# Gathered rows used one block later, mixer outputs normed per head, and a PSUM copy on ScalarE in the output projection

## The chip, the cores and the metric

The kernel runs on one core of a Trainium2 chip. A core has five engines, each with its own in-order instruction queue: TensorE (PE) multiplies matrices into PSUM, VectorE (DVE) and GpSimd (POOL) work elementwise, ScalarE (ACT) applies functions and casts, SyncE (SP) mostly issues transfers. Sixteen DMA engines move data between HBM and SBUF. The metric is the device time of one execution in microseconds (us); less is better.

## The reference

One decoder block with 512 tokens of width 1024, all in float32:

```python
h = rmsnorm(x, norm1_w) * (1 + sc1) + sh1                 # adaLN from c
qa, ka, va, qm, km, vm, om, ip, fp, ga, gm = split_cols(h @ w_in)
y_a = rmsnorm(diff_attention(qa, ka, va), subln_w) * 0.8  # 8 heads of 128
y_m = rmsnorm(mlstm(qm, km, vm, ip, fp), ml_norm_w) * sigmoid(om)   # 8 heads of 128
x = x + gt1 * ((sigmoid(ga) * y_a + sigmoid(gm) * y_m) @ w_out)
h2 = rmsnorm(x, norm2_w) * (1 + sc2) + sh2
x = x + gt2 * peer_ffn(h2, ...)
return rmsnorm(x, final_norm_w)

def peer_ffn(h, w_q, sub_keys, U, V):     # 128 x 128 = 16384 experts
    # 8 heads; the two best-16 lists of product keys give 16 experts for each head
    act = gelu(U[idx] . h)                # one neuron for each of the 8 x 16 picks
    return sum(gate * act * V[idx])
```

## The kernel before

A float32 product is computed as three products of rounded parts: ACT rounds a tile to `hi`, DVE (or POOL) subtracts to get `lo` (`split`, L137 and L138), and PE adds hi x hi, lo x hi and hi x lo in PSUM (`mm3`, L187 to L189).

**The mixers.** Four passes, `hp` = 0 to 3, each compute two heads (`u` = 0, 1) of both mixers. Attention leaves `y_a`, the mLSTM leaves `y_m`, 128 tokens by 256 columns for each of four token tiles `t`. While ACT squares them it collects sums of squares in `ssq`. Then `rstd` turns `ssq` into `rs` (L118 on DVE, a power on POOL at L119), sixteen multiply-multiply instructions (L699, L701) apply `rs` and the gates, and one add (L703) merges the two mixers into `mrg`.

**The output projection.** `merged_t` transposes `mrg` through PE (`mTp`, L601) into `mT`, one k tile for each head. In the last pass, `out_begin` projects k tiles 0 to 5 before that pass's own merge: for each half `j` of the columns and each token tile `t`, a group of 18 matmuls (`wo`) into one PSUM bank of a ring of two, then `o_res = wo * gt1` on DVE (L618) and `x += o_res` on POOL (L619). `out_end` adds k tiles 6 and 7, the last pass's heads. The weights `wo{k}_{j}` are split with their `lo` part on POOL.

**The expert layer.** Scores, top-16 lists and routing tables keep DVE busy from 640 to 940 us. After that, all 16384 experts are computed densely for tokens 128 to 511, in 128 blocks `n1` of 128 experts: a U block (`act`, 24 matmuls of 384 columns, L1000 to L1002), then gelu and the product with the routing weights `W` (`ga`, L1031), and a V block (`y`, 18 matmuls of 512 columns, L1046). Tokens 0 to 127 take the other way: 256 indirect transfers of 512 KB gather the rows that each token picked, 128 of U and then 128 of V. DVE uses a gathered U tile in a dot product (`junk`, L931) and a gathered V tile in an accumulation (`yg`, L941). I call the stretch up to about 1405 us, in which U rows are gathered, the U stretch, and the one from there to 1905 us the V stretch.

**What sets the order.** A scheduler orders the instructions on each engine before the kernel runs; at run time each engine follows its list strictly. Two pins matter here. Each block's gathers are issued on POOL (L925) behind a one-column copy `pace` (L994) that reads that block's `lo_U`, so they start when DVE has made `lo_U` (L992). And a gather needs one of five buffers of the tag `g`, so it waits until DVE has used the tile five gathers back. Each of the `hi` and `lo` weight tiles has two buffers.

Of the kernel before, what the change touches and what calls it, by code (L numbers as in the profile page):

```python
# [61 lines left out]
def block_kernel(ctx: ExitStack, tc: tile.TileContext, a, out, dbg=None):  # L62
# [380 lines left out]
    def attention(hp, y, ssq, between=None):  # L443
# [13 lines left out]
        for u in range(2):  # L457
            if u and between:
                between()
            h = 2 * hp + u  # L460
            us = slice(u * P, (u + 1) * P)

            halves = slice(0, 64), slice(64, P)
            for nm, src in (("q", q_sb), ("k", k_sb)):
                ps = tr_tile(f"{nm}T{h}")
                for t in range(NT):
                    T.transpose(ps[:, t * P:(t + 1) * P], src[:, t, us], ident)
                if nm == "q":
                    for c, r in enumerate(halves):
                        split(qz[0][r, c], qz[1][r, c], ps[r])  # L470
                else:
                    kh, kl = [lp.tile([P, S], F32R, tag=f"kT_{n}", bufs=QB, name=f"kT_{n}") for n in ("hi", "lo")]
                    split(kh, kl, ps)
            rinv = lp.tile([P, NT, 2], F32, tag="rinv", bufs=2, name="rinv")
            for t in range(NT):
                n = (t + 1) * P
                sc = ps_sc.tile([P, 2, S], F32, tag="sc", name="sc")
                for c in range(2):
                    qs = slice(t * P, (t + 1) * P)
                    T.matmul(sc[:, c, 0:n], qz[0][:, c, qs], kh[:, 0:n], start=True, stop=False)  # L480
# [24 lines left out]
            oT = lp.tile([P, S], F32, tag="t2k", bufs=3, name="oT")  # L505
            A.copy(oT, po)
            pt = tr_tile("pt")
            for t in range(NT):
                T.transpose(pt[:, t * P:(t + 1) * P], oT[:, t * P:(t + 1) * P], ident)
            for t in range(NT):  # L510
                V.tensor_scalar(y[:, t, us], pt[:, t * P:(t + 1) * P], rinv[:, t, 0:1], None, op0=OP.mult)
                A.activation(junk, pt[:, t * P:(t + 1) * P], AF.Square, scale=rinv[:, t, 0:1],
                             accum_out=ssq[:, t, u:u + 1])

    def mlstm(hp, y, ssq):

# [50 lines left out]
        for u in range(2):  # L567
# [21 lines left out]
            V.reciprocal(den, den)  # L589
            for c in range(NT):  # L590
                V.tensor_scalar(y[:, c, us], pn[:, c, 0:P], den[:, c:c + 1], None, op0=OP.mult)
                A.activation(junk, pn[:, c, 0:P], AF.Square, scale=den[:, c:c + 1], accum_out=ssq[:, c, u:u + 1])


    x1h, mT = [], []
# [73 lines left out]
    for hp in range(4):  # L669
        js = slice(hp * 256, (hp + 1) * 256)  # L670
        y_a = mrg[:, :, js]
        y_m = lp.tile([P, NT, 256], F32, tag="y_m", bufs=1, name="y_m")
        ssq, rs = [lp.tile([P, 2, NT, 2], F32, tag=n, bufs=2, name=n) for n in ("ssq", "rs")]
        attention(hp, y_a, ssq[:, 0], gate_chain if hp == 0 else None)
        mlstm(hp, y_m, ssq[:, 1])
        mw = lp.tile([P, 256], F32, tag="mw", bufs=1, name="mw")
        A.dma_start(mw, a["ml_norm_w"][js].partition_broadcast(P))

        def gate(tag, off, name):
            g = lp.tile([P, NT, 256], F32, tag=tag, bufs=1, name=name)  # L680
# [12 lines left out]
        rstd(rs.rearrange("p a t u -> p (a t u)"), ssq.rearrange("p a t u -> p (a t u)"), P, 4 * NT)
        ga4 = ga.rearrange("p t (h d) -> p (t h) d", d=P)
        G.tensor_tensor(ga4, ga4, bc(subw[:, None, :], [P, 2 * NT, P]), op=OP.mult)
        for t in range(NT):
            for u in range(2):
                us = slice(u * P, (u + 1) * P)
                V.scalar_tensor_tensor(ga[:, t, us], y_a[:, t, us], rs[:, 0, t, u:u + 1], ga[:, t, us],  # L699
                                       op0=OP.mult, op1=OP.mult)  # L700
                V.scalar_tensor_tensor(gm[:, t, us], y_m[:, t, us], rs[:, 1, t, u:u + 1], gm[:, t, us],  # L701
                                       op0=OP.mult, op1=OP.mult)
        V.tensor_tensor(mrg[:, :, js], ga, gm, op=OP.add)  # L703
    h2_hi, h2_lo = out_end()
    if "x1" in dbg:
        nc.sync.dma_start(dbg["x1"], x1_dram)
# [219 lines left out]
                             in_offset=bass.IndirectOffsetOnAxis(ap=idx0[:, s:s + 1], axis=0))  # L926
        return t_

    def gather_u(s):
        u = gather(a["U"], s)  # L930
        V.scalar_tensor_tensor(junk2, u, 1.0, hrow, op0=OP.mult, op1=OP.mult, accum_out=act[:, s:s + 1])  # L931
        if s == NS - 1:
            A.activation(act, act, AF.Gelu)
            V.tensor_tensor(act, act, gate0, op=OP.mult)

    def gather_v(s):
        v = gather(a["V"], s)
# [39 lines left out]
        V.scalar_tensor_tensor(idx0[:, gs], idg.rearrange("p h k -> p (h k)"), float(KEYS),  # L977
                               idl.rearrange("p h k -> p (h k)"), op0=OP.mult, op1=OP.add)

    gsteps = [(gather_u, s) for s in range(NS)] + [(gather_v, s) for s in range(NS)]  # L980
    h_hi, h_lo = h2_hi[:, :, d0:d0 + XT], h2_lo[:, :, d0:d0 + XT]

    def gstep(n1):
# [2 lines left out]
    def up(n1):  # L986
# [147 lines left out]
```

## Time and profile before

| what | value |
|---|---|
| three timed runs | 1936.87, 1919.65, 1936.19 us (median 1936.19) |
| the profiled execution | 1931.02 us, span 1929.2 us, mean granted clock of PE 0.978 |
| busy share: PE, DVE, ACT, POOL | 94%, 74%, 42%, 36% |
| chain of work that ended last | PE 58%, DVE 18%, DMA 9%, ACT 5%, issue 5%, POOL 4% |

The shares are averages over stages with different limits, so they are read by stage: between 1100 and 1400 us PE never rests, before 940 us DVE is the busiest engine, and later both wait at times. Idle time in a row is the time that the engine sat before the instructions of that group, and the name behind the arrow is what it waited for last. [...]

### The profile page before, as it was taken

How to read it: one execution, taken by the hardware profiler on the slowest of the kernel's cores; microseconds unless marked ns; L12 is line 12 of the kernel's file. 1: busy time of each engine (PE TensorE's matmuls, PEld its weight loads, DVE VectorE, ACT ScalarE, POOL GpSimd, SP SyncE). 2: the span in 40 equal slices, each digit the busy share in tenths (PEclk: the TensorE clock that was granted, in tenths of full speed). 3: DMA queues.
4: the chain of work that ended last, by engine and by line, in shares of the span. 5: the costliest groups of instructions: out<-in, count | busy, mean ns of one | idle time of the engine just before them, and what ended most of it. 6: DMA issues, size and time to landing. Idle time of an engine off the chain costs nothing.

```text
span 1929.2 us, 28915 instructions
## 1 busy us (share of the span) xinstructions
PE 1814.1 (94%) x10751; PEld 1632.3 (85%) x10751; DVE 1428.4 (74%) x2732; ACT 811.1 (42%) x1359; POOL 685.8 (36%) x608
## 2 busy tenths in 40 slices
PE   5999899899998998999699999999999899999997
PEld 4989799798986888999688888899898788888886
DVE  7664746645556799999889888887776667776777
ACT  5565464463562423555434333333333233333332
POOL 2523325234135310331001664565433433334333
PEclk8999999999999999999799999999999999999999
DMA  8422414314222233366794999999986887787883
GB/s 283 129 69 81 138 59 158 112 63 148 71 88 98 75 102 99 117 239 247 265 302 153 339 355 349 317 337 336 323 285 247 276 299 274 273 295 246 321 283 132
DMA packets 160283, 404.26 MB, mean 210 GB/s; under 512 B 14471, under 2 KB 63368, under 8 KB 160142
## 3 DMA queue, kind: packets, MB, share of 16 engines
q1 hardware_dynamic: 117026, 240.91, 38.6%
q0 software_dynamic: 36864, 134.23, 19.0%
q10 hardware_dynamic: 6252, 27.28, 3.6%
q8 instruction: 84, 1.38, 0.3%
q14 instruction: 57, 0.47, 0.1%
HBM read 373.52 MB, written 28.84 MB: 209 GB/s over the span
## 4 chain that ended last, share of the span: by engine, by line
PE 58%; DVE 18%; DMA 9%; ACT 5%; issue 5%; POOL 4%; SPq 0%; DVEq 0%; POOLq 0%; ACTq 0%
PE y L1046 20%; PE act L1002 7%; PE act L1000 7%; PE act L1001 7%; DMA gath<-V,idx 4%; DMA ada_w<-ada_w 3%; POOL gath L925 2%; DVE lo_U L992 2%; DVE ada_acc L219 1%; DVE lo_V L138 1%; PE wps L876 1%; PE wps L877 1%; DVE ga L699 1%; ACT p L489 1%; DVE gm L701 1%
## 5 line engine op out<-in xcount | busy, mean ns | idle before, releaser
L1002 PE MATMUL act<-h_hi,lo_U 128*128 128x384 f32 x1024 | 347.1, 339 | 16.9 <-DVE lo_U L992 16.7
L1000 PE MATMUL act<-h_hi,hi_U 128*128 128x384 f32 x1024 | 345.0, 337 | 2.6 <-ACT ga L1004 2.2
L1001 PE MATMUL act<-h_lo,hi_U 128*128 128x384 f32 x1024 | 344.3, 336 | 0.0
L994 POOL COPY pace<-lo_U 128x1 f32<-128x1 f32 x128 | 99.9, 782 | 572.8 <-DVE lo_U L992 572.1
L941 DVE SCALAR_TENSOR_TENSOR yg<-gath,act,yg 128x1024 f32<-128x1024 f32 x127 | 163.0, 1283 | 111.2 <-DMA gath<-V,idx 110.6
L1046 PE MATMUL y<-lo_V,ahi 128*128 128x512 f32 x762 | 241.2, 397 | 2.6 <-DVE lo_V L138 2.6
L137 ACT CAST hi_V<-raw_V 128x1024 fp32r<-128x1024 f32 x128 | 134.3, 1050 | 245.9 <-PE y L1046 207.3
L1046 PE MATMUL y<-hi_V,alo 128*128 128x512 f32 x762 | 233.9, 395 | 1.0 <-DVE alo L138 1.0
L1046 PE MATMUL y<-hi_V,ahi 128*128 128x512 f32 x762 | 222.4, 397 | 6.0 <-ACT ahi L137 4.2
L925 POOL DMA_INDIRECT gath<-U,idx x128 | 177.1, 1383 | 130.1 <-DVE junk L931 99.3
L1002 PEld LDWEIGHTS act<-h_hi,lo_U 128*128 128x128 f32 x1024 | 192.8, 188 | 25.3 <-DVE lo_U L992 20.6
L1000 PEld LDWEIGHTS act<-h_hi,hi_U 128*128 128x128 f32 x1024 | 192.9, 188 | 8.5 <-ACT ga L1004 3.1
L1001 PEld LDWEIGHTS act<-h_lo,hi_U 128*128 128x128 f32 x1024 | 192.7, 188 | 4.3
L138 DVE TENSOR_TENSOR lo_V<-raw_V,hi_V 128x1024 fp32r<-128x1024 f32 x128 | 155.8, 1219 | 41.9 <-ACT hi_V L137 39.0
L991 ACT CAST hi_U<-raw_U 128x1024 fp32r<-128x1024 f32 x128 | 134.2, 1049 | 111.4 <-PE act L1001 98.6
L137 ACT CAST ahi<-ga 128x384 fp32r<-128x384 f32 x127 | 65.0, 512 | 271.0 <-DVE ga L1031 140.3
L1046 PEld LDWEIGHTS y<-hi_V,alo 128*128 128x128 f32 x762 | 142.5, 187 | 35.4 <-DVE alo L138 1.9
L1046 PEld LDWEIGHTS y<-lo_V,ahi 128*128 128x128 f32 x762 | 142.8, 188 | 35.0 <-DVE lo_V L138 3.6
L992 DVE TENSOR_TENSOR lo_U<-raw_U,hi_U 128x1024 fp32r<-128x1024 f32 x128 | 156.4, 1222 | 19.4 <-ACT hi_U L991 13.3
L1046 PEld LDWEIGHTS y<-hi_V,ahi 128*128 128x128 f32 x762 | 142.0, 189 | 33.3 <-ACT ahi L137 4.8
L925 POOL DMA_INDIRECT gath<-V,idx x128 | 149.4, 1167 | 35.3 <-issue 31.5
L931 DVE SCALAR_TENSOR_TENSOR junk<-gath,hrow 128x1024 bf16<-128x1024 f32 x128 | 156.0, 1219 | 4.4 <-DMA gath<-U,idx 3.5
(465 smaller groups left out, 4134.2 us busy)
## 6 DMA issues: line engine op xcount, KB each, us to landing
raw_U<-UT SPq DMA_DIRECT2D x128, 512.0 KB
raw_V<-V SPq DMA_DIRECT2D x128, 512.0 KB
ada_w<-ada_w SPq DMA_DIRECT2D x96, 256.0 KB
W_dram<-st ACTq DMA_DIRECT2D x24, 960.0 KB
W<-W_dram SPq DMA_DIRECT2D x60, 384.0 KB
raw_wq<-wq SPq DMA_DIRECT2D x16, 512.0 KB
raw_q<-w_in SPq DMA_DIRECT2D x8, 512.0 KB
raw_k<-w_in SPq DMA_DIRECT2D x8, 512.0 KB
```

Of the source, the lines that this page charges most:

```text
L137: A.copy(hi, src)
L138: eng.tensor_tensor(lo, src, hi.bitcast(F32), op=OP.subtract)
L925: G.indirect_dma_start(out=t_, out_offset=None, in_=src, in_offset=bass.IndirectOffsetOnAxis(ap=idx0[:, s:s + 1], axis=0))
L931: V.scalar_tensor_tensor(junk2, u, 1.0, hrow, op0=OP.mult, op1=OP.mult, accum_out=act[:, s:s + 1])
L941: V.scalar_tensor_tensor(yg, v, act[:, s:s + 1], yg, op0=OP.mult, op1=OP.add)
L991: A.copy(hi, raw)
L992: V.tensor_tensor(lo, raw, hi.bitcast(F32), op=OP.subtract)
L994: with tc.issue_after(G.tensor_copy(pace, lo[:, 0:1].bitcast(F32)).ins):
L1000: T.matmul(ps, hi[:, ks], h_hi[:, k], start=(k == 0), stop=False)
L1001: T.matmul(ps, hi[:, ks], h_lo[:, k], start=False, stop=False)
L1002: T.matmul(ps, lo[:, ks], h_hi[:, k], start=False, stop=(k == KD - 1))
L1046: T.matmul(ys[d][j], l[:, tsl], r[:, j * 512:(j + 1) * 512], start=(m == 0 and i == 0), stop=(m == KEYS - 1 and i == 2))
```

## The change

There are three edits.

1. In the expert layer, the issue of a gather and its use come apart. The gathers of block `n1` are issued where they were, but they go on a list `landing`; the list is emptied, and the tiles are used on DVE, right behind `lo_U` of block `n1 + 1` (pinned behind it by `issue_after`). The buffers of tag `g` go from five to six.
2. The norm and merge of a pass are done head by head. `ssq` and `rs` get the head as their first index; per pass there are two `rstd` on 128x8 in place of one on 128x16, and two adds of 128x4x128 in place of one of 128x4x256. The sixteen multiplies are the same.
3. In the eight groups of `out_begin` (`ks[0] == 0`), ACT copies the PSUM bank to `o_res` in SBUF, and DVE multiplies it there by `gt1`. In `out_end` DVE still reads PSUM.

```diff
-NGB = 5
+NGB = 6
...
         o = lp.tile([P, S], F32, tag="t2k", bufs=3, name="o_res")
+        if ks[0] == 0:
+            A.copy(o, ps)
+            ps = o
         V.tensor_tensor(o, ps, gt1[:, j * 512:(j + 1) * 512], op=OP.mult)
...
-        rstd(rs.rearrange("p a t u -> p (a t u)"), ssq.rearrange("p a t u -> p (a t u)"), P, 4 * NT)
...
-        for t in range(NT):
-            for u in range(2):
-                us = slice(u * P, (u + 1) * P)
-                V.scalar_tensor_tensor(ga[:, t, us], y_a[:, t, us], rs[:, 0, t, u:u + 1], ga[:, t, us],
+        for u in range(2):
+            us = slice(u * P, (u + 1) * P)
+            rstd(rs[:, u].rearrange("p a t -> p (a t)"), ssq[:, u].rearrange("p a t -> p (a t)"), P, 2 * NT)
+            for t in range(NT):
+                V.scalar_tensor_tensor(ga[:, t, us], y_a[:, t, us], rs[:, u, 0, t:t + 1], ga[:, t, us],
...
-        V.tensor_tensor(mrg[:, :, js], ga, gm, op=OP.add)
+            V.tensor_tensor(y_a[:, :, us], ga[:, :, us], gm[:, :, us], op=OP.add)
...
-    def gather_u(s):
-        u = gather(a["U"], s)
+    def use_u(s, u):
...
+    landing = []
...
-        V.tensor_tensor(lo, raw, hi.bitcast(F32), op=OP.subtract)
+
+        with tc.issue_after(V.tensor_tensor(lo, raw, hi.bitcast(F32), op=OP.subtract).ins):
+            while landing:
+                f, s, t_ = landing.pop(0)
+                f(s, t_)
         pace = dp.tile([P, 1], F32, tag="pace", bufs=4, name="pace")
         with tc.issue_after(G.tensor_copy(pace, lo[:, 0:1].bitcast(F32)).ins):
-            for f, s in gsteps[gstep(n1):gstep(n1 + 1)]:
-                f(s)
+            for f, n, s in gsteps[gstep(n1):gstep(n1 + 1)]:
+                landing.append((f, s, gather(a[n], s)))
```

The first place is DVE's list in the V stretch, around block 98. Before, `gath_16251` and `gath_16254` are the two gathers of block 98, issued behind `lo_U98`; `gath_16322` is one of block 99.

```order
L992 TENSOR_TENSOR lo_U98_16245<-raw_U_16243,hi_U98_16244 128x1024
L1031 TENSOR_TENSOR ga_16138<-ga_16138,W0_6501 128x384
L138 TENSOR_TENSOR alo_16149<-ga_16138,ahi_16148 128x384
L992 TENSOR_TENSOR lo_U99_16316<-raw_U_16314,hi_U99_16315 128x1024
L1031 TENSOR_TENSOR ga_16212<-ga_16212,W0_6501 128x384
L138 TENSOR_TENSOR alo_16222<-ga_16212,ahi_16221 128x384
L941 SCALAR_TENSOR_TENSOR yg_9155<-gath_16251,act_9154,yg_9155 128x1024
L941 SCALAR_TENSOR_TENSOR yg_9155<-gath_16254,act_9154,yg_9155 128x1024
L941 SCALAR_TENSOR_TENSOR yg_9155<-gath_16322,act_9154,yg_9155 128x1024
L138 TENSOR_TENSOR lo_V98_16286<-raw_V_16284,hi_V98_16285 128x1024
L941 SCALAR_TENSOR_TENSOR yg_9155<-gath_16325,act_9154,yg_9155 128x1024
L992 TENSOR_TENSOR lo_U100_16386<-raw_U_16384,hi_U100_16385 128x1024
```

So before, the blocks come in pairs, and five instructions stand between `lo_U98` and the first use of its gathers. In the changed kernel the list repeats every three blocks. Here `gath_16342` and `gath_16344` belong to block 99, and `gath_16412`, `gath_16414` and `gath_16416` to block 100.

```order
L996 TENSOR_TENSOR lo_U100_16404<-raw_U_16402,hi_U100_16403 128x1024
L943 SCALAR_TENSOR_TENSOR yg_9175<-gath_16342,act_9174,yg_9175 128x1024
L1042 TENSOR_TENSOR ga_16300<-ga_16300,W0_6521 128x384
L943 SCALAR_TENSOR_TENSOR yg_9175<-gath_16344,act_9174,yg_9175 128x1024
L996 TENSOR_TENSOR lo_U101_16477<-raw_U_16475,hi_U101_16476 128x1024
L138 TENSOR_TENSOR alo_16311<-ga_16300,ahi_16310 128x384
L1042 TENSOR_TENSOR ga_16371<-ga_16371,W0_6521 128x384
L943 SCALAR_TENSOR_TENSOR yg_9175<-gath_16412,act_9174,yg_9175 128x1024
L138 TENSOR_TENSOR alo_16381<-ga_16371,ahi_16380 128x384
L943 SCALAR_TENSOR_TENSOR yg_9175<-gath_16414,act_9174,yg_9175 128x1024
L996 TENSOR_TENSOR lo_U102_16548<-raw_U_16546,hi_U102_16547 128x1024
```

Now six instructions, two of them uses of older gathers, stand between `lo_U100` and the first use of its gathers, and a `yg` follows `lo_U100` at once. POOL's own list, one `pace` and two or three gathers for each block, is as before.

The second place is the output projection. On POOL, before, around the last pass's power (`rs<-rs`):

```order
TENSOR_TENSOR rs<-rs,nhalf 128x16
TENSOR_TENSOR x1_0<-x1_0,o_res 128x512
TENSOR_TENSOR lo_wo2_1<-raw_wo2_1,hi_wo2_1 128x1024
TENSOR_TENSOR lo_wo4_1<-raw_wo4_1,hi_wo4_1 128x1024
TENSOR_TENSOR x1_0<-x1_0,o_res 128x512
```

And on POOL in the changed kernel:

```order
TENSOR_TENSOR rs<-rs,nhalf 128x8
TENSOR_TENSOR x1_0<-x1_0,o_res 128x512
TENSOR_TENSOR x1_0<-x1_0,o_res 128x512
TENSOR_TENSOR rs<-rs,nhalf 128x8
TENSOR_TENSOR lo_wo2_1<-raw_wo2_1,hi_wo2_1 128x1024
TENSOR_TENSOR lo_wo4_1<-raw_wo4_1,hi_wo4_1 128x1024
```

The split of `wo2_1` and `wo4_1`, which PE needs for the second half of the columns, now stands behind the second head's power. On PE, the transposes `mTp` of k tiles 6 and 7 stood together behind the first two groups of the second half; now k tile 6 is transposed six matmuls into the first of these groups, and k tile 7 ten matmuls before the end of the two. On ACT at this place the changed kernel has:

```order
COPY o_res<-wo 128x512
ACTIVATE junk_s,ssq<-pn,den 128x128
CAST hi_wo2_1<-raw_wo2_1 128x1024
CAST hi_wo4_1<-raw_wo4_1 128x1024
COPY o_res<-wo 128x512
CAST mT_hi<-mTp 128x512
CAST hi_wo6_0<-raw_wo6_0 128x1024
CAST mT_hi<-mTp 128x512
COPY o_res<-wo 128x512
```

The copies are new; the fourth one, the second copy of this piece, stands ahead of `hi_wo6_0`.

## Rows read from the trace of the kernel before

**Rows 1.** Windows: busy us (x instructions) of PE, PEld, DVE, ACT, POOL, PEclk, DMA share, GB/s

```profile
1100.00:1400.00 300.00, 300.00 (x1452) 263.66 (x1452) 249.66 (x367) 105.78 (x143) 167.85 (x137) 1.00 0.95 339
```

**Rows 2.** Groups of instructions, 1405 to 1905 us: busy, mean ns | idle before, releasers

```profile
L941 DVE SCALAR_TENSOR_TENSOR yg<-gath,act,yg 128x1024 f32<-128x1024 f32 x127 | 163.0, 1283 | 111.2 <-DMA gath<-V,idx 110.6
L1002 PE MATMUL act<-h_hi,lo_U 128*128 128x384 f32 x465 | 157.8, 339 | 12.9 <-DVE lo_U L992 12.8
...
L925 POOL DMA_INDIRECT gath<-V,idx x128 | 149.4, 1167 | 35.3 <-issue 31.5 <-DVE yg L941 3.8
L1046 PE MATMUL y<-lo_V,ahi 128*128 128x512 f32 x336 | 106.1, 396 | 1.4 <-DVE lo_V L138 1.4
L1046 PE MATMUL y<-hi_V,ahi 128*128 128x512 f32 x339 | 105.4, 395 | 1.2 <-ACT ahi L137 0.7 <-ACT hi_V L137 0.5
...
L994 POOL COPY pace<-lo_U 128x1 f32<-128x1 f32 x57 | 31.3, 550 | 278.0 <-DVE lo_U L992 277.4 <-issue 0.5
```

**Rows 3.** Timeline of DVE, 1526 to 1541 us: start, us, instruction [idle before <-releaser]

```profile
1526.25 1.22 DVE L992 TENSOR_TENSOR lo_U<-raw_U,hi_U 128x1024 fp32r<-128x1024 f32 x1
1527.39 0.55 DVE L1031 TENSOR_TENSOR ga<-ga,W 128x384 f32<-128x384 f32 x1
1527.86 1.28 DVE L941 SCALAR_TENSOR_TENSOR yg<-gath,act,yg 128x1024 f32<-128x1024 f32 x1
1529.05 0.55 DVE L138 TENSOR_TENSOR alo<-ga,ahi 128x384 fp32r<-128x384 f32 x1
1529.52 1.28 DVE L941 SCALAR_TENSOR_TENSOR yg<-gath,act,yg 128x1024 f32<-128x1024 f32 x1
...
1539.34 1.28 DVE L941 SCALAR_TENSOR_TENSOR yg<-gath,act,yg 128x1024 f32<-128x1024 f32 x1 [3.39 <-DMA gath<-V,idx]
```

**Rows 4.** Timeline of POOL over the same stretch and to 1545 us

```profile
1527.54 0.44 POOL L994 COPY pace<-lo_U 128x1 f32<-128x1 f32 x1 [4.30 <-DVE lo_U L992]
1528.14 2.30 POOL L925 DMA_INDIRECT gath<-V,idx  x1 [0.16 <-issue]
...
1544.83 0.94 POOL L925 DMA_INDIRECT gath<-V,idx  x1 [0.30 <-issue]
```

**Rows 5.** Timeline of DVE and POOL at 1442 us

```profile
1441.86 1.28 DVE L941 SCALAR_TENSOR_TENSOR yg<-gath,act,yg 128x1024 f32<-128x1024 f32 x1
1442.01 1.17 POOL L994 COPY pace<-lo_U 128x1 f32<-128x1 f32 x1 [8.57 <-DVE lo_U L992]
```

**Rows 6.** Chain of waits, 1405 to 1905 us: start, us, link; two of eleven

```profile
1464.03 5.14 DMA gath<-V,idx
...
1890.27 8.53 DMA gath<-V,idx
```

**Rows 7.** Timeline of PE, 585 to 600 us, in the output projection

```profile
592.11 0.79 PE L187 MATMUL wo<-hi_wo,mT_hi 128*128 128x512 f32 x1 [4.85 <-DVE o_res L618]
...
597.67 0.40 PE L188 MATMUL wo<-lo_wo,mT_hi 128*128 128x512 f32 x1
597.91 0.40 PE L189 MATMUL wo<-hi_wo,mT_lo 128*128 128x512 f32 x1
```

**Rows 8.** Timeline of DVE, 577 to 593 us

```profile
583.17 2.48 DVE L701 SCALAR_TENSOR_TENSOR gm<-y_m,rs,gm 128x128 f32<-128x128 f32 x1
...
587.97 0.34 DVE L701 SCALAR_TENSOR_TENSOR gm<-y_m,rs,gm 128x128 f32<-128x128 f32 x1
...
591.38 0.68 DVE L618 TENSOR_TENSOR o_res<-wo,gt 128x512 f32<-128x512 f32 x1
```

**Rows 9.** Timeline of POOL, 577 to 593 us

```profile
578.94 2.90 POOL L119 TENSOR_TENSOR rs<-rs,nhalf 128x16 f32<-128x16 f32 x1 [0.56 <-DVE rs L118]
...
583.05 4.84 POOL L138 TENSOR_TENSOR lo_wo<-raw_wo,hi_wo 128x1024 fp32r<-128x1024 f32 x2
```

**Rows 10.** Instructions of one line (the query's L767): ns min/median/max, first and last start

```profile
L767 ACT COPY qt<-pr_wq x16: 575/588/595, 646.3 to 746.4; 128x512 f32<-128x512 f32 x16
```

**Rows 11.** Costliest groups of the page: the uses of gathered U rows

```profile
L931 DVE SCALAR_TENSOR_TENSOR junk<-gath,hrow 128x1024 bf16<-128x1024 f32 x128 | 156.0, 1219 | 4.4 <-DMA gath<-U,idx 3.5
```

More of the change, by code (lines that the diff above doesn't have):

```diff
@@ L512, in attention @@
                 A.activation(junk, pt[:, t * P:(t + 1) * P], AF.Square, scale=rinv[:, t, 0:1],
-                             accum_out=ssq[:, t, u:u + 1])
+                             accum_out=ssq[:, u, t:t + 1])
     def mlstm(hp, y, ssq):
@@ L591, in mlstm @@
                 V.tensor_scalar(y[:, c, us], pn[:, c, 0:P], den[:, c:c + 1], None, op0=OP.mult)
-                A.activation(junk, pn[:, c, 0:P], AF.Square, scale=den[:, c:c + 1], accum_out=ssq[:, c, u:u + 1])
+                A.activation(junk, pn[:, c, 0:P], AF.Square, scale=den[:, c:c + 1], accum_out=ssq[:, u, c:c + 1])
     x1h, mT = [], []
@@ L672, in block_kernel @@
         y_m = lp.tile([P, NT, 256], F32, tag="y_m", bufs=1, name="y_m")
-        ssq, rs = [lp.tile([P, 2, NT, 2], F32, tag=n, bufs=2, name=n) for n in ("ssq", "rs")]
-        attention(hp, y_a, ssq[:, 0], gate_chain if hp == 0 else None)
-        mlstm(hp, y_m, ssq[:, 1])
+        ssq, rs = [lp.tile([P, 2, 2, NT], F32, tag=n, bufs=2, name=n) for n in ("ssq", "rs")]
+        attention(hp, y_a, ssq[:, :, 0], gate_chain if hp == 0 else None)
+        mlstm(hp, y_m, ssq[:, :, 1])
         mw = lp.tile([P, 256], F32, tag="mw", bufs=1, name="mw")
@@ L692, in block_kernel @@
             out_begin()
-        rstd(rs.rearrange("p a t u -> p (a t u)"), ssq.rearrange("p a t u -> p (a t u)"), P, 4 * NT)
         ga4 = ga.rearrange("p t (h d) -> p (t h) d", d=P)
         G.tensor_tensor(ga4, ga4, bc(subw[:, None, :], [P, 2 * NT, P]), op=OP.mult)
-        for t in range(NT):
-            for u in range(2):
-                us = slice(u * P, (u + 1) * P)
-                V.scalar_tensor_tensor(ga[:, t, us], y_a[:, t, us], rs[:, 0, t, u:u + 1], ga[:, t, us],
+        for u in range(2):
[3 more added lines that the diff above has]
+                V.scalar_tensor_tensor(ga[:, t, us], y_a[:, t, us], rs[:, u, 0, t:t + 1], ga[:, t, us],
                                        op0=OP.mult, op1=OP.mult)
-                V.scalar_tensor_tensor(gm[:, t, us], y_m[:, t, us], rs[:, 1, t, u:u + 1], gm[:, t, us],
+                V.scalar_tensor_tensor(gm[:, t, us], y_m[:, t, us], rs[:, u, 1, t:t + 1], gm[:, t, us],
                                        op0=OP.mult, op1=OP.mult)
-        V.tensor_tensor(mrg[:, :, js], ga, gm, op=OP.add)
+            V.tensor_tensor(y_a[:, :, us], ga[:, :, us], gm[:, :, us], op=OP.add)
     h2_hi, h2_lo = out_end()
@@ L934, in gather_u, with use_v @@
             V.tensor_tensor(act, act, gate0, op=OP.mult)
-    def gather_v(s):
-        v = gather(a["V"], s)
+    def use_v(s, v):
         if s == 0:
@@ L978, in select_gather @@
                                idl.rearrange("p h k -> p (h k)"), op0=OP.mult, op1=OP.add)
-    gsteps = [(gather_u, s) for s in range(NS)] + [(gather_v, s) for s in range(NS)]
+    gsteps = [(f, n, s) for f, n in ((use_u, "U"), (use_v, "V")) for s in range(NS)]
+    landing = []
     h_hi, h_lo = h2_hi[:, :, d0:d0 + XT], h2_lo[:, :, d0:d0 + XT]
@@ L991, in up @@
         A.copy(hi, raw)
-        V.tensor_tensor(lo, raw, hi.bitcast(F32), op=OP.subtract)
+        with tc.issue_after(V.tensor_tensor(lo, raw, hi.bitcast(F32), op=OP.subtract).ins):
+            while landing:
+                f, s, t_ = landing.pop(0)
+                f(s, t_)
         pace = dp.tile([P, 1], F32, tag="pace", bufs=4, name="pace")
         with tc.issue_after(G.tensor_copy(pace, lo[:, 0:1].bitcast(F32)).ins):
-            for f, s in gsteps[gstep(n1):gstep(n1 + 1)]:
-                f(s)
+            for f, n, s in gsteps[gstep(n1):gstep(n1 + 1)]:
+                landing.append((f, s, gather(a[n], s)))
+        if n1 == KEYS - 1:
+            while landing:
+                f, s, t_ = landing.pop(0)
+                f(s, t_)
         ps = acc_tile("act")[:, 0:XT]
```

## The prediction

> **What bounds the kernel now.** I read it by stage. From 1100 to 1400 us PE is busy for all of 300 us while DVE works 249.66 [rows 1]: nothing is to be won there. In the V stretch PE does rest, and the groups say on what: 12.9 us before the first matmuls that need `lo_U`, 1.4 before those of `lo_V`, 1.2 before `ahi` [rows 2]. `lo_U` is late because DVE takes its list in order, and DVE sits 111.2 us in front of `yg`, nearly all of it for gathered V rows [rows 2]. The timeline shows one such turn: after `lo_U` DVE works on, then waits 3.39 us for a landing, and what stands behind that `yg`, the next `lo_V` and `lo_U` with PE behind them, waits too [rows 3]. It is a loop: `lo_U`, `pace`, gathers on POOL, landing, `yg`, next `lo_U`. The chain of waits has eleven such landings, the first and last of them 5.14 and 8.53 us long, eight of them over 7 [rows 6]. A second place where PE rests is the output projection, 4.85 us for an `o_res` [rows 7].
>
> **The loop before.** `pace` appears 57 times in these 500 us [rows 2], so a block takes 8.77 us; without PE's 15.5 us of rest it would be 8.50, thus 17.0 for a pair and 25.5 for three. DVE's steps, from start to start, are 1.14 for `lo_U` (I take the same for `lo_V`), 0.47 each for `ga` and `alo`, 1.19 for `yg` [rows 3]. With 128 gathers in 57 blocks that is 2 x 1.14 + 2 x 0.47 + 2.25 x 1.19 = 5.9 us a block, so a pair leaves DVE 17.0 - 11.8 = 5.2 us for waiting. Between `lo_U98` and the first use of its gathers stand five instructions, 1.14 + 4 x 0.47 = 3.0 us. The way round takes `pace` 0.44, one gather's issue 0.94 [rows 4], some 0.25 between the steps, and the landing L. DVE's wait is then L + 1.63 - 3.0 = L - 1.4: 3.7 us at 5.14, 7.1 at 8.53. From L = 6.6 on it is more than the 5.2 that the pair has, and eight of the eleven are longer. Their overrun, about 1.4 us at a landing near 8, comes to 11 us, close to the 12.9 that the row shows.
>
> **The loop after.** Three blocks leave DVE 25.5 - 17.7 = 7.8 us. Between `lo_U100` and the first use of its gathers stand two `yg`, a `lo_U`, an `alo` and two `ga`: 2 x 1.19 + 1.14 + 3 x 0.47 = 4.9 us. Two things get dearer. `pace` no longer has a `ga` behind it on DVE but a `yg`, and where that was so it took 1.17 us, not 0.44 [rows 4, 5]. A gather's issue, 0.94 at a quiet moment, took 2.30 while DVE ran `yg`, `alo`, `yg` [rows 3, 4]; its mean is 1.17 [rows 2]. With that mean the wait is L + 0.25 + 1.17 + 1.17 - 4.9 = L - 2.3, which is 6.2 us at the longest landing shown; with 2.30 it is 7.3. Both fit into 7.8. So nearly all of the 12.9 us goes. The 2.6 us for `lo_V` and `ahi` stay, as they hang on no gather. I take **-12 us**; the ends are 0 (next part) and -15.5.
>
> [...]
>
> **Sixth buffer.** It adds no transfer. In the U stretch it lets POOL send a gather earlier; PE has no rest there to give back. I cost it at nothing; the cover is that DVE waits for gathered U rows for only 3.5 us in all [rows 11].
>
> **Output projection.** PE's rest of 4.85 us ends when DVE gets to `o_res`, which stood behind sixteen multiplies [rows 7, 8]. After it PE ran slow: 13 steps took 597.67 - 592.11 = 5.56 us where a step at 597.67 takes 0.24, so 2.4 us more; the granted clock in these us is the lower of its two levels. Together 7.25 us are at stake. With the copy on ACT, 0.59 us as other PSUM copies of this size take [rows 10], the bank is free without DVE. ACT's eight copies cost 4.7 us, beside PE. What is late next is POOL: the split of `wo2_1` and `wo4_1`, 2.42 each, starts at 583.05 right behind the power and an add [rows 9]; now it stands behind a second power. The power on 128x16 took 2.90 [rows 9]; for 128x8 I have no row and bound it by 0 and 2.9. PE meets `lo_wo2_1` 8 matmuls into the second half, with no slack to see, so I give back all of 2.9: **-4 us**, ends 0 and -7.25.
>
> **Norm and merge.** Each pass has one more small instruction on DVE, one more power on POOL and one more add. In the first three passes PE works on projections meanwhile and I cost them at **+1 us** in all, ends 0 and +4 (four powers of at most 2.9, a third of them uncovered).
>
> **End.** The last landing of 8.53 us starts at 1890.27 [rows 6], behind PE's last blocks. The uses move a little; **-1 us**, ends 0 and -3.
>
> **Sum.** 1931.0 - 12 - 4 + 1 - 1 = **1915 us**, against the profiled execution. That one lies 5.2 us below the median of the runs, 1936.19, and 11.4 above the fastest, 1919.65, so it stands for them.
>
> **Rivals.**
>
> *The landings keep setting the pace.* If POOL's steps beside DVE all take the longer value and landings lengthen as gathers bunch, the wait is L - 1.2 and passes 7.8 from L = 9.0. The longest shown is 8.53, which speaks against it; for it speaks that only the landings on the chain are seen, and that a late use now holds up three blocks. With 3 to 5 us gained in the V stretch and 3 elsewhere: 1931 - 7 = **1924**.
>
> *The output projection gains nothing.* `mTp` of k tile 6 and 7 now stands among the matmuls of the second half, and PE takes its list in order. The second head's multiplies start behind the second power, together with the split of `wo2_1`; beside a split one multiply took 2.48 us, not 0.34 [rows 8, 9]. And `o_res` used to read PSUM and took 0.68; now both inputs lie in SBUF, and it may wait for a split in the same way, up to 2.4 us, ahead of the merges. If k tile 7's merge is 4 us late, PE rests there instead, and the lower clock comes back: +2 in place of -4, so **1921**. [...]
>
> *Slower: the U stretch, with PE at 100%, starts to rest.* DMA is at 0.95 there and moves 339 GB/s [rows 1]. One more gather of 512 KB in flight stands for 0.524 MB / 339 GB/s = 1.5 us. If each block's `raw_U` or `raw_V` comes that much later and has no reserve, 300 / 8.5 = 35 blocks lose 1.5 us each, 53 us: 1915 + 53 = **1968**. It makes the kernel slower by over 1% from 1.2 us a block on. Against it: the bytes are the same, so a delay once paid isn't paid again, and PE never rests there today.
>
> *All of it is gained and the rests at the end too:* -15.5 - 7.25 - 3, and 1931 becomes **1905**.
>
> *That the change doesn't do what it says* is out for the order: six instructions stand there in place of five. For the merge it is part of the second rival.
>
> **How the numbers follow.** Chances: the forecast 0.50, its own range 1907 to 1922; landings 0.22; output projection 0.13; all gained 0.08; slower 0.07. The range 1902 to 1930 leaves out the slower rival and the outer ends. A change of 1% is about what a measurement of this kernel can tell, so faster means under 1916.8, slower over 1955.6, both against the median. The forecast is just under the first bound: I give faster 0.31 of its 0.50, all of the last case, 0.04 of the output projection's and 0.03 of the landings' case, 0.46. Slower is 0.06. The rest, 0.48, is within 1%.
>
> **What would show it.** Right: DVE's rest before `yg` in the V stretch falls from 111 us to under 80, PE's rest before `lo_U` from 12.9 to under 4, `pace` there takes 1.1 to 1.2 us after a `yg`; PE's 4.85 us before the sixth projection group (second half, second tile) is gone, and what rest is left there names `lo_wo` or `mTp`. Wrong: PE's rest before `lo_U` stays above 8, or PE rests between 1100 and 1400 us, or PE's rest at 585 to 600 us only changes its name.

## The result: 1907.8 us, 1.4% faster

The changed kernel takes 1907.84 us (median of four runs, 1904.39 to 1910.03) against 1934.83 for the kernel before beside it: a ratio of 0.9864, 95% interval 0.9827 to 0.9900. A second set of runs (e9) gave 0.9861 (0.9836 to 0.9887). The forecast was 1915 in a range of 1902 to 1930, so the time lies in the range, and the way was right. By the profiles, 1931.02 became 1904.39, with a span of 1902.6 us: 26.6 us gained where the forecast had summed up 16. Medians and ratios leave out one execution of the kernel of e5, which took 4759.17 us.

The windows of the changed kernel answer to [rows 1]; columns as there.

```profile
1100.00:1400.00 300.00, 300.00 (x1455) 263.94 (x1455) 247.87 (x362) 106.77 (x145) 163.42 (x134) 1.00 0.93 331
1400.00:1500.00 100.00, 100.00 (x503) 90.16 (x502) 72.61 (x79) 34.70 (x48) 40.88 (x40) 1.00 0.89 304
1500.00:1600.00 100.00, 100.00 (x503) 90.24 (x502) 73.74 (x78) 35.20 (x48) 40.41 (x40) 1.00 0.83 282
...
1700.00:1800.00 100.00, 100.00 (x503) 90.10 (x502) 72.06 (x76) 34.97 (x48) 45.41 (x40) 1.00 0.86 288
```

PE no longer rests anywhere between 1100 and 1800 us. The groups of 1405 to 1905 us answer to [rows 2].

```profile
L943 DVE SCALAR_TENSOR_TENSOR yg<-gath,act,yg 128x1024 f32<-128x1024 f32 x127 | 162.8, 1282 | 52.4 <-DMA gath<-V,idx 51.9
L1013 PE MATMUL act<-h_hi,lo_U 128*128 128x384 f32 x455 | 152.5, 335 | 0.0
L929 POOL DMA_INDIRECT gath<-V,idx x127 | 149.9, 1180 | 31.8 <-issue 31.8
L1057 PE MATMUL y<-lo_V,ahi 128*128 128x512 f32 x348 | 109.5, 395 | 0.0
...
L1001 POOL COPY pace<-lo_U 128x1 f32<-128x1 f32 x56 | 41.5, 742 | 237.4 <-DVE lo_U L996 237.4
```

DVE's rest before `yg` fell from 111.2 us to 52.4, PE's before `lo_U` from 12.9 to none. What is left of DVE's rest up to 1850 us costs nothing, as PE doesn't rest there. The timeline shows the step that answers to [rows 3 to 5]:

```profile
1519.88 1.28 DVE L943 SCALAR_TENSOR_TENSOR yg<-gath,act,yg 128x1024 f32<-128x1024 f32 x1
1520.04 1.17 POOL L1001 COPY pace<-lo_U 128x1 f32<-128x1 f32 x1 [11.69 <-DVE lo_U L996]
...
1521.37 1.10 POOL L929 DMA_INDIRECT gath<-V,idx  x1 [0.16 <-issue]
...
1522.78 0.94 POOL L929 DMA_INDIRECT gath<-V,idx  x1 [0.31 <-issue]
...
1526.89 1.30 DVE L943 SCALAR_TENSOR_TENSOR yg<-gath,act,yg 128x1024 f32<-128x1024 f32 x1 [0.63 <-DMA gath<-V,idx]
...
1529.40 0.45 POOL L1001 COPY pace<-lo_U 128x1 f32<-128x1 f32 x1 [1.53 <-DVE lo_U L996]
```

`pace` takes 1.17 us where a `yg` follows `lo_U` and 0.45 where a `ga` does, as was said; but the two uses of the gathers that this first `pace` released wait 0.63 and 0.11 us, where those in the turn of [rows 3] waited 1.53 and 3.39.

**Where the 26.6 us of span came from.** Pieces of PE's work can be found in both traces. The table gives, for each kernel, how many us before the kernel before it got to the same piece. "Dense 300", "700" and "1090" are three points at which PE has done the same amount of the expert layer's matmuls; counting `act` and `y` alone, at their steps of 0.173 and 0.233 us, they lie at 218, 619 and 1009 of 1068 us.

| piece of PE's work | before, at us | after | after, 2nd profile | e1 | e2 | e3 | e4 | e5 | e10 | e11 | e12 |
|---|---|---|---|---|---|---|---|---|---|---|---|
| second pass, first scores | 217.3 | -1.9 | -2.7 | -0.5 | 1.9 | 1.9 | -0.8 | -2.3 | -1.3 | 3.8 | 3.2 |
| projection, first matmul | 565.8 | 5.6 | 5.5 | -0.6 | 10.3 | 3.5 | -1.0 | 2.4 | 6.9 | 4.4 | 1.1 |
| projection, last matmul | 622.0 | 4.9 | 5.3 | -0.5 | 10.3 | 8.4 | 3.9 | 2.6 | 12.8 | 4.1 | 2.2 |
| first `act` | 739.1 | 2.1 | 2.8 | -0.5 | 10.7 | 3.6 | -1.2 | 3.0 | 10.5 | 4.3 | 1.4 |
| dense 300 | 1040.9 | 4.8 | 4.9 | -0.9 | 10.1 | 3.9 | -3.3 | 4.5 | 9.8 | 5.6 | 2.7 |
| dense 700 | 1443.7 | 4.7 | 5.6 | -5.6 | 7.2 | 0.2 | -5.7 | 5.0 | 11.1 | 7.0 | -0.7 |
| dense 1090 | 1854.4 | 24.2 | 25.0 | 13.5 | 6.3 | 0.9 | 13.8 | 24.5 | 30.5 | 15.1 | -3.4 |
| end | 1929.2 | 26.6 | 27.4 | 16.0 | 7.1 | 3.8 | 16.7 | 27.3 | 32.9 | 16.8 | -0.6 |

Read it by differences down a column, as single profiles scatter by some us: e7 and e11, whose lists are the same, differ by 4.5 us in the V stretch. In the changed kernel 19.5 us come from the V stretch, 2.4 from the end, 7.5 from the passes (between their second and the projection), nothing from the projection, and 2.8 are lost in the norm behind it. Three smaller differences, -1.9 at the start, -0.7 in the projection and 2.7 about the first dense blocks, cancel.

**The projection after** answers to [rows 7]. PE's list in the changed kernel:

```profile
584.73 0.39 PE L187 MATMUL wo<-hi_wo,mT_hi 128*128 128x512 f32 x1
591.22 1.09 PE L601 MATMUL mTp<-ident,mrg 128*128 128x128 f32 x4 [6.11 <-DVE mrg L707]
...
592.53 0.63 PE L189 MATMUL wo<-hi_wo,mT_lo 128*128 128x512 f32 x1
592.96 0.63 PE L187 MATMUL wo<-hi_wo,mT_hi 128*128 128x512 f32 x1
```

The wait of 4.85 us for `o_res` is gone, and one of 6.11 us for the second head's merge stands there, with steps of 0.43 us after it as before, at a granted clock of 0.50 in both traces. That is the lower of the two levels that these traces show; the other is 1.00. The timeline of DVE says why that merge is late; it answers to [rows 8].

```profile
579.73 2.47 DVE L703 SCALAR_TENSOR_TENSOR ga<-mrg,rs,ga 128x128 f32<-128x128 f32 x1 [2.93 <-POOL rs L119]
582.12 2.48 DVE L705 SCALAR_TENSOR_TENSOR gm<-y_m,rs,gm 128x128 f32<-128x128 f32 x1
...
584.79 0.68 DVE L622 TENSOR_TENSOR o_res<-o_res,gt 128x512 f32<-128x512 f32 x1
...
586.93 2.42 DVE L705 SCALAR_TENSOR_TENSOR gm<-y_m,rs,gm 128x128 f32<-128x128 f32 x1
...
589.80 0.68 DVE L138 TENSOR_TENSOR mT_lo<-mTp,mT_hi 128x512 fp32r<-128x512 f32 x1
590.40 0.67 DVE L707 TENSOR_TENSOR mrg<-ga,gm 128x512 f32<-128x512 f32 x1
```

DVE waits 2.93 us for the second head's power, and three of its multiplies take 2.4 us beside POOL's splits in place of 0.34. An `o_res` and an `mT_lo` stand ahead of the merge too, but take their plain 0.68.

### The profile page after: what moved, and what is told of

It is laid out like the page before. It is cut to its first block, busy times and chain, and to the rows that moved or that the text cites. A ratio compares the mean times of both kernels' runs of the same rounds, so it can differ in the third digit from the quotient of the medians.

```text
span 1902.6 us, 28969 instructions
## 1 busy us (share of the span) xinstructions
PE 1806.3 (95%) x10751; PEld 1630.8 (86%) x10751; DVE 1431.7 (75%) x2740; ACT 817.4 (43%) x1367; POOL 697.0 (37%) x612
## 3 DMA queue, kind: packets, MB, share of 16 engines
q0 software_dynamic: 36864, 134.23, 19.5%
## 4 chain that ended last, share of the span: by engine, by line
PE 72%; DVE 14%; ACT 5%; DMA 4%; issue 3%; POOL 1%; SPq 0%; DVEq 0%; POOLq 0%; ACTq 0%
PE y L1057 26%; PE act L1013 9%; PE act L1011 9%; PE act L1012 9%; DMA ada_w<-ada_w 3%; DVE ada_acc L219 1%; PE wps L880 1%; PE wps L881 1%; PE pr_wq L188 1%; PE pr_wq L187 1%; PE pr_wq L189 1%; ACT p L489 1%; DVE ga L703 1%; DVE onehot L871 1%; PE pt_gm L187 1%
## 5 line engine op out<-in xcount | busy, mean ns | idle before, releaser
L1001 POOL COPY pace<-lo_U 128x1 f32<-128x1 f32 x128 | 107.9, 844 | 548.5 <-DVE lo_U L996 548.4
L1057 PE MATMUL y<-hi_V,alo 128*128 128x512 f32 x762 | 229.7, 395 | 0.0
L1057 PE MATMUL y<-hi_V,ahi 128*128 128x512 f32 x762 | 217.8, 397 | 4.7 <-ACT ahi L137 3.5
L943 DVE SCALAR_TENSOR_TENSOR yg<-gath,act,yg 128x1024 f32<-128x1024 f32 x127 | 162.8, 1282 | 52.4 <-DMA gath<-V,idx 51.9
L996 DVE TENSOR_TENSOR lo_U<-raw_U,hi_U 128x1024 fp32r<-128x1024 f32 x128 | 156.5, 1223 | 16.3 <-ACT hi_U L994 11.1
```

Of the source, the lines that this page charges most:

```text
L996: with tc.issue_after(V.tensor_tensor(lo, raw, hi.bitcast(F32), op=OP.subtract).ins):
L1057: T.matmul(ys[d][j], l[:, tsl], r[:, j * 512:(j + 1) * 512], start=(m == 0 and i == 0), stop=(m == KEYS - 1 and i == 2))
```

## The experiments

The theory after the result had three parts: the V stretch gains because a gather's use stands farther behind its `lo_U` on DVE's list; the passes gain from the norm per head; the copy on ACT gains nothing, because of the rest at `mTp` or because of what follows the projection. The rivals were the sixth buffer for the first, scatter for the second, and for the third that the rest at `mTp` is a loss by itself. Runs e1 to e5 and e8 take the change apart.

### e1 to e4: one edit alone, or one left out

```diff
# e1: the first edit alone
-NGB = 5
+NGB = 6
...
+        with tc.issue_after(V.tensor_tensor(lo, raw, hi.bitcast(F32), op=OP.subtract).ins):
+            while landing:
# e2: the second edit alone
+            rstd(rs[:, u].rearrange("p a t -> p (a t)"), ssq[:, u].rearrange("p a t -> p (a t)"), P, 2 * NT)
# e3: the third edit alone
+            A.copy(o, ps)
+            ps = o
# e4: the changed kernel, second edit undone
-            rstd(rs[:, u].rearrange("p a t -> p (a t)"), ssq[:, u].rearrange("p a t -> p (a t)"), P, 2 * NT)
+        rstd(rs.rearrange("p a t u -> p (a t u)"), ssq.rearrange("p a t u -> p (a t u)"), P, 4 * NT)
```

> Only the first edit: gathered rows used behind the next block's lo_U, six buffers; norm, merge and output projection as before. Theory (the gain of 27 us in the profiles lies in the V stretch, where PE's rest before lo_U fell): PE stays at 100% from 1400 to 1800 us, the stage ledger gains 18 to 21 us between 1405 and 1890 us and 2 more at the end, nothing ahead of 640 us; time 1908 to 1916. Rival (a part of the gain comes from the norm per head, whose passes ran 5.6 us earlier): the same 20 us here and the passes unchanged, so 1911 to 1915, and the norm alone then gains 4 to 6. Rival (the gain needs all three edits): under 10 us, 1921 or more.

Measured: 1907.91 us, ratio 0.9879 (0.9850 to 0.9908). The V stretch gains 19.1 us (from -5.6 to 13.5), the end 2.5, the passes nothing. The first edit is the change's gain, nearly alone. Between dense 300 and 700 this profile loses 4.7 us that the changed kernel doesn't lose; e2 to e4 lose 2.4 to 3.7 there, so it isn't the gathers' use. Each of these profiles has one longer rest of PE there, at a `y` that waits for ACT's `hi_V` (3.0 us in e1, 1.2 in the kernel before and the changed one), and a stretch at the lower clock behind it, 6.8 us in e1 and 3.4 in e2 to e4, that the other two lack. Half of 6.8 and the 1.8 us of rest make 5.2, about what was lost. What delays `hi_V` I have not followed.

> Only the second edit: norm and merge per head. Theory (the per-head norm shifts the passes by a few us, and then loses in the output projection, since PE's transposes of the last head stand among the matmuls of the second half and wait for a merge that POOL's splits delay): the passes end 3 to 6 us earlier at 555 us, PE rests 3 to 7 us before mTp, and the expert layer starts between 2 us earlier and 3 us later than before; time within 6 us of the kernel before. Rival (the earlier passes come from elsewhere, the norm costs its instructions): passes end within 1 us of before or later. Rival (it gains at the merge, as the edit's form suggests): no PE rest over 2 us between 580 and 600 us and a gain of 8 or more.

Measured: 1928.51 us, 0.9984 (0.9957 to 1.0011), so the time alone doesn't tell it from no change. Its profile gains 8.4 us in the passes and keeps them, so the expert layer starts 10.7 us earlier. Of the theory the first half holds, with more than the 3 to 6 us that it gave, and the second fell: PE rests at `o_res` as before, 4.6 us, and under 1 us at `mTp`. The transposes stand early in this list too (k tile 7 fourteen matmuls into the two groups), but behind that rest at `o_res`; the rest at `mTp` shows where the copy has taken away the one at `o_res`.

> Only the third edit: ACT copies the first eight projection groups out of PSUM. In this order both mTp stay behind the first two groups of the second half. Theory (the copy does free the bank, and the rest of 6.1 us at mTp in the changed kernel belongs to the norm per head and not to the copy): PE's rest of 4.85 us before the second group of the second half is gone, no rest over 2 us stands between 580 and 600 us, and the projection ends 4 to 7 us earlier against the start of its first group. Rival (o_res from SBUF collides with POOL's splits and delays the merge): PE rests 4 us or more at mTp or at wo, and the projection gains under 2 us.

Measured: 1932.18 us, 1.0018 (0.9997 to 1.0039). The projection gains 4.9 us, as the theory had it, and the norm behind it loses 4.8. PE's waits in 600 to 650 us of this run (engine, line, waited for: us in total, times, longest):

```profile
PE h2p L663 <- DVE x L656: 2.8, 1, 2.8
PE h2p L663 <- issue: 2.6, 1, 2.6
PE pr_wq L188 <- DVE h_lo L668: 2.4, 1, 2.4
```

In the kernel before these are 2.0, 1.5 and 0.2 us. An earlier end of the projection is mostly waited away there, at DVE's steps of the norm, `x` and `h_lo`.

> The changed kernel with the second edit undone (one norm and merge per pass), the first and third kept. Theory (the per-head norm gains some 5 us in the passes and loses 6 at mTp): time within 4 us of the changed kernel, 1904 to 1912, but the ledger differs: no gain at 555 us, 4 to 7 us in the projection, 19 in the V stretch. Rival (the passes' gain is not from the norm): this kernel keeps it and is 4 to 7 us faster than the changed one, 1901 to 1904.

Measured: 1907.96 us, 0.9881 (0.9849 to 0.9913). As expected: the passes gain nothing, the projection 4.9 us, the norm behind it loses 5.1, the V stretch gains 19.5. So without the norm per head the copy is worth nothing either.

### e5: the first two edits, without the copy

```diff
-        if ks[0] == 0:
-            A.copy(o, ps)
-            ps = o
```

> The changed kernel with the third edit undone: the first two edits alone, projection groups read from PSUM by DVE. Theory (the copy's 6 us in the projection are given back in the norm that follows, with the norm per head it even brings a rest of 6 us at mTp, so it is worth nothing or less): the passes end 5 to 10 us earlier than in the kernel before, that lead is kept through the projection and the norm, V stretch 19; time 1898 to 1907, no slower than the changed kernel's 1908 and perhaps 5 faster. Rival (the copy is worth its 4 us in the changed kernel): 1910 to 1914.

Measured: 1903.70 us, 0.9847 (0.9816 to 0.9878): no slower than with the copy, and not told from it either. The passes gain 4.7 us here.

### e6, e9 and e10: the transposes pinned

```diff
+        return T.matmul(ps, l_lo, r_hi, start=False, stop=stop)
...
+        pins.append(mm.ins)
...
-        merged_t(6, 8, tr_tile)
+        with tc.issue_after(pins[5]):
+            merged_t(6, 8, tr_tile)
```

`pins[5]` is the last matmul of the second group of the second half.

> The changed kernel with the transposes of k tiles 6 and 7 pinned behind the second group of the second half, where the kernel before has them. Theory (the rest of 6.1 us at mTp is PE's list meeting a late merge, but what follows, the norm of x, is bound by DVE and ACT and not by the projection's end): the rest at mTp falls under 2 us and the projection ends 4 to 6 us earlier, yet the first scores come at most 2 us earlier; time within 3 us of the changed kernel's. Rival (the rest at mTp cost the change its gain): scores and the whole kernel 5 to 6 us earlier, 1901 to 1903.

> The changed kernel as it is, once more, on the same chip as the next run, to compare the two directly. Theory (the rest at mTp is the changed kernel's own loss): 4 to 8 us slower than the pinned one. Rival (the earlier difference of 6 us came from the two chips or from the passes' scatter): within 2 us of it.

> The changed kernel with both transposes pinned, once more, beside the changed kernel on the same chip. Theory: 1898 to 1904, 4 to 8 us under the changed kernel's median, and by its profile the projection ends 5 to 6 us earlier than in the changed kernel's, against its own start. Rival: within 2 us of the changed kernel.

Measured: e6 1901.27 us, 0.9833 (0.9804 to 0.9862). On one chip, e9 (the changed kernel) 1905.49 us and e10 (pinned) 1897.47, 0.9830 (0.9802 to 0.9857); their profiled spans are 1901.8 and 1896.3. PE's wait in e10, 556 to 650 us, that answers to the 6.11:

```profile
PE mTp L601 <- DVE mrg L711: 0.9, 1, 0.9
```

My theory for e6 fell. In e10 the projection gains 5.9 us, and of them only 2.3 are lost in the norm behind it; 3.6 stay, where e9 loses 2.7 over both. The rest at `mTp` did cost some 6 us. The pinned kernel is the fastest of all here, 8 us under the changed one by the medians of six runs each and 6 by their means, with an interval of about 0 to 12. Whether the copy pays once the transposes are pinned is not shown by time: e6, with it, and e5, without it, ran on one chip and are 2.4 us apart. By the ledger, projection and norm together gain 3.6 us in e10 and 0.6 in e5.

### e7, e8 and e11: the pin and the sixth buffer

```diff
# e7: the first edit without its pin
-        with tc.issue_after(V.tensor_tensor(lo, raw, hi.bitcast(F32), op=OP.subtract).ins):
-            while landing:
+        V.tensor_tensor(lo, raw, hi.bitcast(F32), op=OP.subtract)
+        while landing:
# e8: the first edit with
+NGB = 5
# e11: the kernel before with
+NGB = 6
```

> The first edit alone without its pin: the uses are still written behind the next block's lo_U, six buffers, but nothing holds them there on DVE's list; then 2.6 to 4.5 us of DVE's work stand between a lo_U and the first use of its gathers in the worst blocks, as in the kernel before, where the pinned list has 4.9 at least. Theory (the distance on DVE's list is what pays): PE's rest before lo_U in the V stretch stays at 8 to 15 us, DVE's before yg at 85 or more, the V stretch gains under 8 us of the 19; time 1920 to 1934. Rival (the sixth buffer pays, by letting POOL send earlier): V stretch gains 15 or more, 1906 to 1914.

> The first edit alone with five buffers, pinned. The list on DVE keeps 4.5 us or more between lo_U and the first use. Theory (distance pays, the sixth buffer matters little): V stretch gains 14 to 20 us, time 1907 to 1918. Rival (later uses hold buffers longer, and with five POOL's gathers wait for one): POOL rests over 30 us before gathers for yg in the V stretch, landings come late, and under 8 us are gained, 1920 or more.

> The kernel before with six buffers in place of five and nothing else. The lists of all engines are those of the unpinned run, which gained 12.6 us in the V stretch with PE resting 4.6 us before lo_U. Theory (that list is better, whatever in it does it): V stretch gains 8 to 14 us again, time 1914 to 1925. Rival (that profile had lucky landings): V stretch gains under 5 us and PE rests 9 us or more before lo_U; 1925 or more.

Measured: e8, with the pin and five buffers, 1913.55 us, 0.9883 (0.9847 to 0.9919), 19.4 us gained in the V stretch. So the pin with five buffers brings the gain of the V stretch, and where the pin is, the sixth buffer adds nothing. But e7 took 1918.70, 0.9918 (0.9892 to 0.9944), with 12.6 us gained in the V stretch, and e11, whose lists are the same, 1916.86, 0.9926 (0.9903 to 0.9950), with 8.1: a part of the gain comes without the pin. Neither the theory of e7 nor its rival holds as it stood. By time e1 and e8 gain 23 us each and e7 and e11 16 and 14, each to within 5 to 7 us, so that what the pin adds to the list of six buffers is told mainly by the profiles. The waits of e7 and of e11 in 1405 to 1890 us:

```profile
DVE yg L939 <- DMA gath<-V,idx: 95.0, 59, 4.6
...
PE act L1009 <- DVE lo_U L992: 4.6, 5, 1.5
```

```profile
DVE yg L941 <- DMA gath<-V,idx: 99.3, 58, 5.3
...
PE act L1002 <- DVE lo_U L992: 8.3, 11, 1.4
```

and of e8:

```profile
DVE yg L939 <- DMA gath<-V,idx: 48.2, 35, 3.5
```

With six buffers and no pin DVE waits for the landings nearly as long as before, but PE's rests are 1.5 us at most, not 4.7. With the pin DVE's waits halve. The sixth buffer's effect goes by way of the scheduler, which plans another list: in the kernel before a gather of this stretch waited for a buffer only twice, 3.8 us in all, and in e11 still twice, 3.7 us. What in that list shortens the rests I could not settle. The distance between a `lo_U` and the first use of its gathers, counted in steps as the prediction counts it, is hardly it: it is most often 3.0 us in e11 and in the kernel before, and 4.8 and 4.6 us in the mean of the blocks; the pin makes that 7.0, and 4.9 at the least.

### e12: one power for both heads

```diff
-            rstd(rs[:, u].rearrange("p a t -> p (a t)"), ssq[:, u].rearrange("p a t -> p (a t)"), P, 2 * NT)
+        rstd(rs.rearrange("p u a t -> p (u a t)"), ssq.rearrange("p u a t -> p (u a t)"), P, 4 * NT)
```

> The second edit without its two powers: multiplies and adds head by head as in the change, but one rstd on all of ssq for both heads, behind the second head's sums. Theory (the passes gain because the first head's power is done early and its eight multiplies fill the time in which POOL works on the second): DVE waits 2 us or more for rs at the end of each pass again, PE's rest before pr_m for v_lo is 4 us or more in all as in the kernel before, and the passes gain under 3 us between the second pass's start and the projection. Rival (splitting the multiplies and the add does it): PE's rest for v_lo is under 2.5 us and the passes gain 6 or more.

Measured: 1934.43 us, 1.0013 (0.9993 to 1.0032); the passes lose 2.1 us. PE's wait for `v_lo` in 190 to 556 us (5.9 in the kernel before), and DVE's for `rs` up to 600 (4.3 before):

```profile
PE pr_m L187 <- DVE v_lo L138: 4.4, 4, 1.4
```

```profile
DVE ga L699 <- POOL rs L119: 4.6, 4, 2.8
```

The longest wait for `rs`, 2.8 us, is the second pass's; it is the same in the kernel before and gone in the six profiles with two powers. The theory had 2 us or more in each pass, and that is so in this one alone, here as before. So the split of the multiplies and the add does not pay without the first head's early power. It is not without effect, though: `v_lo` costs 3.3 us here from the second pass's first scores on, against 5.3 before, and a rest of 4.7 us for `ada_acc` (1.2 before), which the theory did not have, uses that up. Over all twelve runs and the first profile, the passes from the second to the projection gain 4.7 to 8.4 us in the six profiles with two powers, and -2.1 to 1.6 in the seven without.

## Why the prediction was right, and where it was not

**The V stretch: mechanism right, size too small.** The forecast was -12 with -15.5 as its outer end, measured -19.5. The loop was the one described, and the rest before `lo_U` went to nothing, as did the 2.6 us that I had left standing for `lo_V` and `ahi`. The rest was not the whole price: PE's ten rests in 1405 to 1850 us sum to 14.7 us, and 4.8 more went with them. After the longest, 4.73 us, PE ran at the lower clock, granted 0.50, for 3.4 us, where a matmul's step was 0.32 us and not 0.17, so about 1.5 us. That is the only stretch at the lower clock there. Most of the other 3 us lies around the rests at the upper clock: the profile counts a rest from a matmul's modelled end, 0.16 us behind the point where the next one starts in flow, and the first step after it was 0.10 us longer, so 0.26 us ten times. The term to add is what a rest costs after it has ended; I used it for the projection and forgot it here.

**The landings as the first rival** is out: DVE's waits halved. The landings were not short: in the changed kernel they came 4.5 to 10.4 us after the start of the issue, 7.4 in the median. The issue did not all go to the longer value either: of the first issues behind a `pace`, those that began beside `ga` or `alo` took 1.10 us, those that began beside a `yg` 1.83 to 2.30, as in the turn that I had read, and those with DVE idle 0.96; the second issue mostly took 0.94, beside a `yg` too, as the one at 1526.94 us did, 0.93 within a `yg` of 1.30. The mean is 1.18 against 1.17.

**Output projection: the step failed.** I gave back 2.9 us for a late split of the weights, and PE did not wait for `lo_wo` at all. What came was the second rival's mechanism, PE's list meeting the second head's merge too early, 6.11 us, and the forecast of -4 became 0. That is the last of the signs that I had named for being wrong: the rest at 585 to 600 us only changed its name. And I had not asked whether the norm behind the projection could use an earlier end: e3 and e4 show that it gives back 5 us of 5 where the merge is undivided, and e10 2.3 of 5.9.

The rival's other half, that `o_res` from SBUF is held up, did not come ahead of the merge here: 0.68 us in the rows above, and 1.06 at most in the changed kernel, beside an add of POOL's. In e3 the longest took 1.76 us; no `o_res` that read PSUM took more than 0.69 in the kernel before or in the changed one.

**Norm and merge: the step had the wrong sign.** I priced its instructions at +1 us, with 0 as the best end, and asked for no gain; the passes gained 7.5. The trace of the kernel before held it. The timeline of DVE at the end of the second pass, before:

```profile
327.78 0.17 DVE L118 TENSOR_SCALAR rs<-ssq 128x16 f32<-128x16 f32 x1
...
331.44 2.48 DVE L699 SCALAR_TENSOR_TENSOR ga<-mrg,rs,ga 128x128 f32<-128x128 f32 x1 [2.80 <-POOL rs L119]
...
342.68 0.68 DVE L138 TENSOR_TENSOR v_lo<-pt_v,v_hi 128x512 fp32r<-128x512 f32 x1
```

and PE, which waits for that `v_lo`:

```profile
343.41 0.50 PE L187 MATMUL pr_m<-hT_hi,hi_m 128*128 128x512 f32 x1 [2.05 <-DVE v_lo L138]
```

In the changed kernel DVE at the same place:

```profile
326.12 0.74 DVE L118 TENSOR_SCALAR rs<-ssq 128x8 f32<-128x8 f32 x1 [0.53 <-ACT junk_s L592]
326.79 0.34 DVE L703 SCALAR_TENSOR_TENSOR ga<-mrg,rs,ga 128x128 f32<-128x128 f32 x1
...
328.63 0.34 DVE L705 SCALAR_TENSOR_TENSOR gm<-y_m,rs,gm 128x128 f32<-128x128 f32 x1
...
330.16 2.49 DVE L703 SCALAR_TENSOR_TENSOR ga<-mrg,rs,ga 128x128 f32<-128x128 f32 x1
...
340.42 0.68 DVE L138 TENSOR_TENSOR v_lo<-pt_v,v_hi 128x512 fp32r<-128x512 f32 x1
```

Eight multiplies of the first head fill the 2.80 us in which DVE waited for the power, and the next pass's `v_lo` comes 2.3 us earlier, though this profile was 1.9 us behind when the pass began. In the third pass of the kernel before, DVE waits only 0.17 us for `rs`, yet PE waits 3.26 us for `v_lo`: there DVE's `lo_vm` split ran beside one of POOL's and took 3.38 us, and so it is in the six other profiles with an undivided merge (3.36 to 3.38; in e12 1.49). In the changed kernel, and in the other five profiles with two powers, the same split takes 1.22, and PE doesn't wait. From the second pass's first scores to the projection, PE's waits for `v_lo` thus fall from 5.3 us to none, in all six profiles with two powers.

That is not the whole of the 5 to 8 us, and the two don't simply add up. Other rests come in the place of these, so PE's rests in this stretch fall from 18.9 us to 13.6 in the changed kernel, but only to 17.2 in e2, and are 19.3 in e5. The clock does the rest in those two: the stretches at the lower level, 17.1 us in all in the kernel before, are 3.4 us in e2 and 6.8 in e5. At half the clock, 0.50 granted for 1.00, the difference is worth 6.8 and 5.1 us, an estimate, and with the rests it makes 8.5 and 4.7; the table has 8.4 and 4.7. In the changed kernel's first profile they are 17.1 us as before, and 2 of its 7.5 us stay unexplained.

**Sixth buffer, U stretch and end.** The buffer is worth nothing where the pin is, as was said (e8), though alone it is worth 8 to 13 us. The U stretch costs and gains nothing (4.8 at dense 300, 4.7 at dense 700), so the slower rival is out. The end gained 2.4 us, not 1. **The chances**: 0.48 stood on within 1% and 0.46 on faster; it was faster by 1.4%. The sum of errors: 7.5 too little for the V stretch, 8.5 on the norm's side and 1.4 at the end, against 4 too much for the projection and 2.8 for the norm behind it. Two terms, the V stretch and the norm, lie beyond the ends that were given, and the norm behind the projection had no term. So it is in part luck that the time fell in the range: errors of 17.4 us one way met 6.8 the other way.

## What to carry to other kernels

Where a loop runs through a transfer, write down the work that the waiting engine has between the issue's trigger and the use, and compare it with the landing: moving the closest uses from some 3.0 to 4.9 us behind the trigger took PE's rests away, though half of DVE's waits are still there. Price a rest with the slow steps after it (4.8 us on 14.7 of rest in the V stretch here), and before you count a rest that goes, ask what the next stage waits for. When a step is made earlier, look at what else moved up in the in-order lists: one transposition put ten matmuls too early cost as much as the copy could gain.

## What the runs showed of the hardware

A one-column copy on POOL took 0.19 us with DVE idle (`pace` in the kernel before). In the changed kernel it took 0.45 beside a `ga` of 0.55 at 1529.25 us and 1.17 beside a `yg` of 1.28 at 1519.88, and both times it ended 0.05 us after DVE's instruction. DVE's multiply of 128x128 took 0.34 us alone and 2.4 beside a split on POOL, in three of the eight of the last head's norm in the changed kernel. A DVE split of 128x1024, `lo_vm`, took 3.38 us beside one of POOL's at 473.79 us of the kernel before, and 1.22 without at 468.24 us of the changed one.
